# The four products after the gates with the tokens as the stationary operand and 512 weight columns moving

## The chip, the cores and the metric

The kernel runs on one core of one Trainium2 chip. The metric is device time in microseconds (us) of one execution; lower is better. In the text **PE** is TensorE, **PEld** its weight loads, **DVE** VectorE, **ACT** ScalarE, **SP** the queue that issues transfers. Lnnn is a line of the kernel before; where a line is one of the changed kernel, the text says so.

## The reference, cut to what matters

One block with 256 latent tokens and 256 context tokens, 2048 channels wide. All inputs are float32. The part that the change touches:

```python
u = hn @ w_in + b_in                      # 7 slices of 2048 columns: a, g, z_c, xr, z_r, gc, gr
y_conv = (swish(layernorm(conv(a * sigmoid(g)))) * silu(z_c)) @ w_conv_out
y_rnn = ((hf + hb) * silu(z_r)) @ w_rnn_out     # hf, hb: scans over the tokens, both directions
y = sigmoid(gc) * y_conv + sigmoid(gr) * y_rnn
out = rmsnorm(x + gt * (y @ w_o), final_g)      # gt: a gate vector from silu(c) @ w_ada
```

So five products of 256 tokens by a 2048 x 2048 matrix stand at the end: **gr** and **gc** (columns of w_in), **rnn** (w_rnn_out), **conv** (w_conv_out) and **o** (w_o). The four first feed the merge `y`, the fifth takes it.

## The kernel before

**Products.** A float32 product is made of three of the type float32r: each operand is split into a leading part and a remainder (`xh`, `xl` of the tokens, `whi`, `wlo` of the weights), and `whi*xh + whi*xl + wlo*xh` is summed in PSUM. A *block* is 1 MB of weights (two halves of 512 KB, tiles `raw`). `stage_load` asks for a block three ahead; `stage_split(s + 2, h)` makes `whi` on ACT (L180) for the block two ahead, and `wlo` on DVE (L185) for the half block before that one. There are four buffers of each kind, so a `whi` can be made only when PE has done the half block two blocks earlier.

**Two forms of a block.** In `slot` (L573, products at L234) a block is 128 output channels: 16 channel tiles of weights are stationary one after the other, the 256 tokens move, 48 products of 256 columns, and the result has the channels on the partitions. In the loop of w_o (L928, `o_mms`, products at L912) four blocks together make a *chunk* of 512 output columns: a 128 x 128 tile of the tokens is stationary, 512 weight columns move, 24 products per block, two sums (one per 128 tokens), and the result has the tokens on the partitions. The operand of either form has the channels on the partitions.

**Order.** After the first part (adaLN, the recurrent branch) the blocks run as a and g (32 blocks), z_c, gr, rnn, gc, conv, o (16 each). Everything is emitted in program order; each engine works through its own instructions in that order. DVE's other work is spread by hand: `side` is a list of closures with a cost in nominal us, and each half block runs `budget / 2` of it (`run_side`, L411). The list holds first the 480 taps of the depthwise convolution (L660), then LayerNorm (`ln_center`, `ln_a`, `ln_b`), then the 16 splits of the conv operand into `xh`, `xl` (`ln_split`, L774: ACT, then DVE), then four memsets of the gt sums (L763) and `gt_start`. What is left of the list after gc runs at once (L866 to L868). `gt_step` (L820, 64 of them) sums the vector gt on DVE from weights of its own (`gtraw`); its first step also needs a row `bgt`, loaded (L814) after the memsets.

**Results.** gr and gc go from PSUM through ACT's tanh with the bias as a per-partition operand (L851, L863); rnn is multiplied in by one DVE instruction per block (L855); conv by two (L875, L876), and the merged tile is split at once into `xh`, `xl` for w_o (L877). All of these are 128 x 256. The two last w_o blocks run one token tile after the other, and `finish` normalises and stores (L943 to L949).

Of the kernel before, what the change touches and what calls it, by code (L numbers as in the profile page):

```python
# [81 lines left out]
def block_kernel(ctx, tc, xcat, xtok, fgrow, par, wada, wgt, bgt, wearly, wall, wgate, out):  # L82
# [55 lines left out]
    # softplus(-lam) = max(-lam, 0) + log1p(exp(-|lam|)), log1p(e) = 2 atanh(e / (2 + e))  # L138
# [55 lines left out]
    def rsqrt(dst, tmp, src):  # L194
        # dst = (src + eps) ** -0.5, one Newton step on the table's value
# [7 lines left out]
    def ada_mms(acc, raw, rnd, n):  # L203
        # raw holds 8 // n channel tiles of 128 n columns of w_ada
# [7 lines left out]
    def ada_fin(row, part, k0, n):  # L212
        # sums of the four partial rows, channels to partitions
# [11 lines left out]
    def stat_mm(acc, x, i):  # L225
        # mean over channels: four column groups of the array take every fourth tile
# [10 lines left out]
    with ExitStack() as st:  # L237
# [28 lines left out]
        # with the tokens on the partitions, and back  # L266
# [27 lines left out]
        def products(m, ks, ws):  # L294
# [7 lines left out]
            # partial sums, in the end where the input's first tiles were  # L302
# [282 lines left out]
    s = 0  # L585
# [438 lines left out]
```

## Time and profile before

| | us |
|---|---|
| median of 3 runs | 1146.66 (1145.42 to 1146.89) |
| span of the profiled execution | 1142.0 |
| its own time | not listed apart from the span; the runs lie 3.4 to 4.9 above it |
| PE busy | 1121.5 |
| DVE busy | 924.9 |
| ACT busy | 615.1 |
| moved by transfers | 233.70 MB, mean 205 GB/s |

The span runs from the first to the last instruction that the profiler recorded. Busy times are of each engine alone and overlap. Two figures stand for the length of an instruction: the mean of one, in which neighbours on an engine can overlap, and the busy time over the count, in which they do not. PE is read best from the chain of waits, which gives pieces of uninterrupted work with their number of products.

### The profile page before, as it was taken

To read this page: it belongs to the slowest core of one execution; us is meant where nothing else is said; L and a number is where in the kernel's file an instruction comes from. 1 tells how busy PE (TensorE), PEld (TensorE's weight loads), DVE (VectorE), ACT (ScalarE), POOL (GpSimd) and SP (SyncE) were. 2 spreads that over 40 slices of the span, in tenths; PEclk is the share of its full clock that TensorE was granted. 3 is DMA by queue.
4 is the path that set the end of the run, shared out by engine and by line. 5 is a ranking of instruction groups with operands and counts; after the bars stand their busy time and mean duration, and the time that the engine had idled before them with its cause. 6 is when DMAs were issued, how large, how long until landed. Compare 5 with 4: busy or idle time off the path is not lost.

```text
span 1142.0 us, 20720 instructions
## 1 busy us (share of the span) xinstructions
PE 1121.5 (98%) x8316; PEld 1010.7 (88%) x8316; DVE 924.9 (81%) x1528; ACT 615.1 (54%) x838; POOL 0.2 (0%) x4
## 2 busy tenths in 40 slices
PE   6999999999999999999999999999999999999996
PEld 3777778777798989999999999999999999999885
DVE  5555588789879888899998989999985977888885
ACT  3222279777888877644454444443335854444443
POOL 0000000000000000000000000000000000000000
PEclk9999999999999999999999999999999999999999
DMA  9998444233346555465555555555554569888772
GB/s 376 400 409 324 189 134 134 102 125 125 106 141 196 160 167 164 143 209 184 185 185 171 183 183 185 175 183 178 181 188 150 169 205 324 316 310 285 268 279 93
DMA packets 67635, 233.70 MB, mean 205 GB/s; under 512 B 7505, under 2 KB 11729, under 8 KB 67153
## 3 DMA queue, kind: packets, MB, share of 16 engines
q1 hardware_dynamic: 67538, 232.37, 59.5%
q8 instruction: 65, 1.06, 0.4%
q14 instruction: 32, 0.26, 0.1%
HBM read 230.25 MB, written 2.10 MB: 203 GB/s over the span
## 4 chain that ended last, share of the span: by engine, by line
PE 98%; DVE 1%; DMA 0%; ACT 0%; issue 0%; ACTq 0%; SPq 0%; DVEq 0%
PE acc L234 72%; PE o L912 8%; PE xr L234 6%; PE gate L472 5%; PE ada L209 2%; PE part L234 2%; PE ms L228 1%; DMA hbuf<-in_xcat_dram 0%; PE tp L216 0%; PE mps L228 0%; PE gps L833 0%; PE vps L228 0%; DVE sq L259 0%; DVE wlo L171 0%; PE tot L279 0%
## 5 line engine op out<-in xcount | busy, mean ns | idle before, releaser
L234 PE MATMUL acc<-xh,whi 128*128 128x256 f32 (+1 forms) x2176 | 566.8, 296 | 0.0
L234 PE MATMUL acc<-xl,whi 128*128 128x256 f32 (+1 forms) x2176 | 552.3, 289 | 0.0
L180 ACT ACTIVATE whi<-raw 128x1024 fp32r<-128x1024 f32 x304 | 321.1, 1058 | 351.0 <-PE acc L234 277.3
L234 PEld LDWEIGHTS acc<-xh,whi 128*128 128x128 f32 x2176 | 416.7, 192 | 17.8 <-issue 9.3
L234 PEld LDWEIGHTS acc<-xl,whi 128*128 128x128 f32 x2176 | 416.9, 192 | 12.5 <-issue 7.7
L185 DVE TENSOR_TENSOR wlo<-raw,whi 128x1024 fp32r<-128x1024 f32 x304 | 371.0, 1223 | 70.0 <-ACT whi L180 66.3
L234 PE MATMUL acc<-xh,wlo 128*128 128x256 f32 (+1 forms) x2176 | 319.0, 289 | 0.0
L234 PEld LDWEIGHTS acc<-xh,wlo 128*128 128x128 f32 x2176 | 288.2, 192 | 5.0
L660 DVE SCALAR_TENSOR_TENSOR cv<-hbuf,pt,cv 128x196 f32<-128x196 f32 (+14 forms) x480 | 185.9, 451 | 13.0 <-ACT cv L651 12.6
L461 DVE SCALAR_TENSOR_TENSOR xc<-xr,pt,xc 128x510 f32<-128x510 f32 (+2 forms) x96 | 71.0, 742 | 0.2
L472 PE MATMUL gate<-xc,gw 128*128 128x512 f32 x128 | 60.0, 592 | 0.0
L820 DVE SCALAR_TENSOR_TENSOR zc<-gtraw,csil,zc 128x512 f32<-128x512 f32 x64 | 47.9, 748 | 5.4 <-DMA gtraw<-in_wgt_dram 4.7
L234 PE MATMUL xr<-xh,whi 128*128 128x512 f32 x96 | 40.4, 421 | 0.4 <-ACT xh L170 0.4
L912 PE MATMUL o<-whi,xh 128*128 128x512 f32 x128 | 40.6, 399 | 0.0
L498 DVE TENSOR_TENSOR_SCAN tr<-a,ti 128x512 f32<-128x512 f32 x32 | 39.1, 1223 | 0.7
L333 ACT ACTIVATE row<-ada 128x128 f32<-128x128 f32 (+1 forms) x22 | 7.2, 326 | 60.2 <-PE ada L209 60.2
L912 PE MATMUL o<-whi,xl 128*128 128x512 f32 x128 | 39.5, 389 | 0.0
L912 PE MATMUL o<-wlo,xh 128*128 128x512 f32 x128 | 39.4, 389 | 0.0
L234 PE MATMUL xr<-xl,whi 128*128 128x512 f32 x96 | 37.7, 392 | 0.2 <-DVE xl L171 0.2
L472 PEld LDWEIGHTS gate<-xc,gw 128*128 128x128 f32 x128 | 22.8, 189 | 17.0 <-issue 13.9
L234 PE MATMUL xr<-xh,wlo 128*128 128x512 f32 x96 | 37.4, 390 | 0.0
L209 PE MATMUL ada<-adaraw,csil 128*32 128x128 f32 (+1 forms) x704 | 32.5, 324 | 1.1 <-DVE sh L218 0.9
(169 smaller groups left out, 838.1 us busy)
## 6 DMA issues: line engine op xcount, KB each, us to landing
raw<-in_wall_dram SPq DMA_DIRECT2D x304, 512.0 KB, 3.5
adaraw<-in_wada_dram SPq DMA_DIRECT2D x64, 512.0 KB, 8.5
gtraw<-in_wgt_dram SPq DMA_DIRECT2D x32, 512.0 KB, 3.9
raw<-in_wearly_dram SPq DMA_DIRECT2D x16, 512.0 KB, 9.9
gw<-in_wgate_dram SPq DMA_DIRECT2D x32, 128.0 KB, 3.2
hbuf<-in_xcat_dram SPq DMA_DIRECT2D x2, 1024.0 KB, 7.1
cv<-in_xtok_dram SPq DMA_DIRECT2D x4, 512.0 KB, 5.8
out_dram<-cv SPq DMA_DIRECT2D x6, 256.0 KB, 2.6
```

Of the source, the lines that this page charges most:

```text
L180: A.activation(out=hi, in_=raw, func=AF.Copy)
L185: V.tensor_tensor(out=lo, in0=raw, in1=hi.bitcast(F32), op=SUB)
L209: PE.matmul(out=acc[g:g + 32, :w], lhsT=csil[:, k, :], rhs=raw[:, w * q:w * q + w], start=(k < 4), stop=(k >= KT - 4), tile_position=(0, g))
L228: PE.matmul(out=acc[32 * q:32 * q + 32, :], lhsT=ones[:, :32], rhs=x, start=(i < 4), stop=(i >= KT - 4), tile_position=(0, 32 * q))
L234: PE.matmul(out=acc, lhsT=w, rhs=x, start=(first and i == 0), stop=(last and i == n - 1))
L333: A.activation(out=row, in_=acc, func=AF.Copy)
L461: V.scalar_tensor_tensor(out=o, in0=i, scalar=w, in1=o, op0=MUL, op1=ADD)
L472: PE.matmul(out=acc, lhsT=u["gw"][:, c:c + 128], rhs=u["xc"], start=True, stop=True)
L498: V.tensor_tensor_scan(out=r(u["tr"]), data0=r(u["a"]), data1=r(u["ti"]), initial=0.0, op0=MUL, op1=ADD)
L660: V.scalar_tensor_tensor(out=o, in0=i, scalar=hdw[:, m * CW + j:m * CW + j + 1], in1=o, op0=MUL, op1=ADD)
L820: V.scalar_tensor_tensor(out=gt_chunk(c), in0=gt_raw[0][:, 512 * (k % 2):512 * (k % 2) + 512], scalar=csil[:, k, 0:1], in1=gt_chunk(c), op ...
L912: PE.matmul(out=acc, lhsT=y[:, k, 1, P * i:P * i + P], rhs=w[:, 512 * kk:512 * kk + 512], start=(k == 0 and w is hi and y is xh), stop=(k ...
```

## The change

gr, rnn, gc and conv take the form that w_o has: `chunk_mms` is the former `o_mms` with a choice of the operand's half, `chunk_slot` is `slot` with it, and `chunks` runs four chunks of four blocks. The weights of the four matrices are laid out for it outside the kernel's time. The gates and the merge then have the tokens on the partitions. The biases of gr and gc lie along the free axis now: they are loaded as rows spread over all partitions (`bias_load`, one buffer of 512 columns) and added on DVE before the tanh. The evacuations are 128 x 512, two per chunk. The merged value has to get back to channels on the partitions for w_o: `turn` makes two 128 x 128 transposes on PE into PSUM and splits from there. The budgets of side work go from 2.9 to 2.5 (gr, rnn) and from 2.6 to 2.3 (gc), and the squares of LayerNorm have 6 buffers instead of 8. The number of weight blocks, their splits and their loads are as before.

```diff
-BUD_XR, BUD_ZR, BUD_R, BUD, BUD_LN = 8.0, 2.7, 3.0, 2.9, 2.6
+BUD_XR, BUD_ZR, BUD_R, BUD, BUD_Y, BUD_LN = 8.0, 2.7, 3.0, 2.9, 2.5, 2.3
+GBB = 1
+CHUNKED = ("gr", "rnn", "gc", "conv", "o")
...
-    seq += [("in", BGR + m) for m in range(KT)]
-    seq += [("rnn", m) for m in range(KT)]
-    seq += [("in", BGC + m) for m in range(KT)]
-    seq += [("conv", m) for m in range(KT)]
-    seq += [("o", m) for m in range(KT)]
+    for a in CHUNKED:
+        seq += [(a, m) for m in range(KT)]
...
+    def chunk_mms(acc, s, seg, kq, h, i):
+        hi, lo = parts[s, h]
+        for w, y in ((hi, xh), (hi, xl), (lo, xh)):
+            for kk in range(2):
+                k = 4 * kq + 2 * h + kk
+                PE.matmul(out=acc, lhsT=y[:, k, seg, P * i:P * i + P], rhs=w[:, 512 * kk:512 * kk + 512],
+                          start=(k == 0 and w is hi and y is xh), stop=(k == KT - 1 and w is lo))
+    def chunk_slot(s, seg, accs, kq, budget):
+        stage_load(s + 3)
+        for h in range(2):
+            for i in range(2):
+                chunk_mms(accs[i], s, seg, kq, h, i)
+            del parts[s, h]
+            stage_split(s + 2, h)
+            run_deferred()
+            run_side(budget / 2)
...
-        sq = tp2.tile([P, T], F32, tag="sq", name="sq", bufs=8)
+        sq = tp2.tile([P, T], F32, tag="sq", name="sq", bufs=6)
...
-    for m in range(KT):
-        acc = slot(s, lat, T, BUD)
-        A.activation(out=p2[:, m], in_=acc, func=AF.Tanh, scale=0.5, bias=hbin[:, BGR + m:BGR + m + 1])
-        s += 1
-    for m in range(KT):
-        acc = slot(s, ctxp, T, BUD)
-        V.scalar_tensor_tensor(out=p2[:, m], in0=p2[:, m], scalar=1.0, in1=acc, op0=ADD, op1=MUL)
-        s += 1
+    p2v = p2.rearrange("p k t -> p (k t)")
+    tgv = vb.rearrange("p k t -> p (k t)")
+    def piece(v, c, i):
+        return v[:, 2048 * i + 512 * c:2048 * i + 512 * c + 512]
+    def bias_load(j, c):
+        t = tp2.tile([P, 512], F32, tag="gbias", name="gbias", bufs=GBB)
+        SP.dma_start(out=t, in_=bass.AP(brow.tensor, 2048 * j + 512 * c, [[0, P], [1, 512]]))
+        return t
+    def chunks(seg, budget, evac, before=None):
+        nonlocal s
+        for c in range(4):
+            accs = [psum(f"y{c}{i}") for i in range(2)]
+            for kq in range(4):
+                if before:
+                    before(c, kq)
+                chunk_slot(s, seg, accs, kq, budget)
+                s += 1
+            for i in range(2):
+                evac(c, i, accs[i])
+    def gate(v, c, i, acc, bias):
+        g = piece(v, c, i)
+        V.tensor_tensor(out=g, in0=acc, in1=bias, op=ADD)
+        A.activation(out=g, in_=g, func=AF.Tanh, scale=0.5)
+    gbias = {}
+    def before_gr(c, kq):
+        if kq == 1:
+            gbias[c] = bias_load(0, c)
+    chunks(1, BUD_Y, lambda c, i, acc: gate(p2v, c, i, acc, gbias[c]), before_gr)
+    def evac_rnn(c, i, acc):
+        g = piece(p2v, c, i)
+        V.scalar_tensor_tensor(out=g, in0=g, scalar=1.0, in1=acc, op0=ADD, op1=MUL)
+    chunks(0, BUD_Y, evac_rnn)
     ln["rnn"] = True
     ln_splits()
-    for m in range(KT):
-        acc = slot(s, lat, T, BUD_LN)
-        while m not in conv_done:
-            run_side(0.5)
-        A.activation(out=tgc[:, m], in_=acc, func=AF.Tanh, scale=0.5, bias=hbin[:, BGC + m:BGC + m + 1])
-        gt_steps(GTG)
-        s += 1
+    def before_gc(c, kq):
+        if kq == 1:
+            gbias[c] = bias_load(1, c)
+        gt_steps(GTG)
+    def evac_gc(c, i, acc):
+        while any(m not in conv_done for m in (8 * i + 2 * c, 8 * i + 2 * c + 1)):
+            run_side(0.5)
+        gate(tgv, c, i, acc, gbias[c])
+    chunks(1, BUD_LN, evac_gc, before_gc)
     while side or any(queue):
         run_side(1e9)
         run_deferred()
-    for m in range(KT):
-        acc = slot(s, ctxp, T, 0.0)
-        gt_steps(GTN)
-        if m % 2:
-            o_load(m // 2)
-        V.scalar_tensor_tensor(out=tgc[:, m], in0=tgc[:, m], scalar=1.0, in1=acc, op0=ADD, op1=MUL)
-        V.tensor_tensor(out=p2[:, m], in0=p2[:, m], in1=tgc[:, m], op=ADD)
-        split(xh[:, m, 1, :], xl[:, m, 1, :], p2[:, m])
-        s += 1
+    def turn(m):
+        tps = psum("tps")[:, :T]
+        for i in range(2):
+            PE.transpose(tps[:, P * i:P * i + P], p2v[:, 2048 * i + P * m:2048 * i + P * m + P], pall("ident"))
+        split(xh[:, m, 1, :], xl[:, m, 1, :], tps)
+    turns = deque()
+    def before_conv(c, kq):
+        gt_steps(GTN)
+        m = 4 * c + kq
+        if m % 2:
+            o_load(m // 2)
+        if turns:
+            turn(turns.popleft())
+    def evac_conv(c, i, acc):
+        g, t = piece(p2v, c, i), piece(tgv, c, i)
+        V.scalar_tensor_tensor(out=t, in0=t, scalar=1.0, in1=acc, op0=ADD, op1=MUL)
+        V.tensor_tensor(out=g, in0=g, in1=t, op=ADD)
+        if i:
+            turns.extend(range(4 * c, 4 * c + 4))
+    chunks(0, 0.0, evac_conv, before_conv)
...
-    def o_mms(acc, s, kq, h, i):
-        hi, lo = parts[s, h]
-        for w, y in ((hi, xh), (hi, xl), (lo, xh)):
-            for kk in range(2):
-                k = 4 * kq + 2 * h + kk
-                PE.matmul(out=acc, lhsT=y[:, k, 1, P * i:P * i + P], rhs=w[:, 512 * kk:512 * kk + 512],
-                          start=(k == 0 and w is hi and y is xh), stop=(k == KT - 1 and w is lo))
...
-                    o_mms(accs[i], s, kq, h, i)
+                    chunk_mms(accs[i], s, 1, kq, h, i)
                 del parts[s, h]
                 stage_split(s + 2, h)
                 gt_steps(GTO)
+                if turns:
+                    turn(turns.popleft())
```

The order of the instructions shows the change at three places. **DVE at the end of gc** (`xl<-cv` are the splits of the conv operand, `MEMSET zc` clears the sums of gt, L820, in the changed kernel L842, are gt's steps, L898 of the changed kernel adds gc's bias for the last chunk). Before:

```order
L171 TENSOR_TENSOR xl<-cv,xh 128x256 x3
L185 TENSOR_TENSOR wlo<-raw,whi 128x1024
L171 TENSOR_TENSOR xl<-cv,xh 128x256 x2
L763 MEMSET zc 128x512
L185 TENSOR_TENSOR wlo<-raw,whi 128x1024
L763 MEMSET zc 128x512 x2
L185 TENSOR_TENSOR wlo<-raw,whi 128x1024
L763 MEMSET zc 128x512
L185 TENSOR_TENSOR wlo<-raw,whi 128x1024
L820 SCALAR_TENSOR_TENSOR zc<-gtraw,csil,zc 128x512 x2
```

and now:

```order
L187 TENSOR_TENSOR wlo<-raw,whi 128x1024
L173 TENSOR_TENSOR xl<-cv,xh 128x256 x3
L898 TENSOR_TENSOR hbuf<-y_9185,gbias 128x512
L898 TENSOR_TENSOR hbuf<-y_9186,gbias 128x512
L173 TENSOR_TENSOR xl<-cv,xh 128x256 x13
L785 MEMSET zc 128x512 x4
L842 SCALAR_TENSOR_TENSOR zc<-gtraw,csil,zc 128x512 x2
L187 TENSOR_TENSOR wlo<-raw,whi 128x1024 x2
L842 SCALAR_TENSOR_TENSOR zc<-gtraw,csil,zc 128x512 x2
```

Before, the splits and memsets stood between the weights' remainders, a few at a time; now 13 splits, four memsets and two steps of gt stand in one run ahead of the next two remainders.

**PE between two conv blocks** (`acc` are the sums of two neighbouring blocks). Before:

```order
L234 MATMUL acc_10591<-xh,whi 128x256
L234 MATMUL acc_10591<-xl,whi 128x256
L234 MATMUL acc_10591<-xh,wlo 128x256 x8
L234 MATMUL acc_10660<-xh,whi 128x256
L234 MATMUL acc_10660<-xl,whi 128x256
```

and now, at the end of the first conv chunk (`y_9408` is its second sum, `y_9575` the first sum of the next chunk, `tps` the transposes, L936 of the changed kernel):

```order
L581 MATMUL y_9408<-whi,xh 128x512 x2
L581 MATMUL y_9408<-whi,xl 128x512 x2
L581 MATMUL y_9408<-wlo,xh 128x512 x2
L936 MATMUL tps<-pt,p_5033 128x128 x2
L581 MATMUL y_9575<-whi,xh 128x512 x2
L581 MATMUL y_9575<-whi,xl 128x512 x2
L581 MATMUL y_9575<-wlo,xh 128x512 x2
```

The next block's products followed directly; now the first two transposes, which read the merged chunk, stand ahead of the next chunk's products. The same stands at the two other chunk ends of conv; the other 13 pairs of transposes stand between blocks, or, after conv, between half blocks of w_o.

**DVE in the last w_o chunk** (ssq and ms are the norm's sums, L896 and in the changed kernel L974 the first instruction on a finished sum). Before:

```order
L896 SCALAR_TENSOR_TENSOR hbuf<-o_12056,zc 128x512
L897 TENSOR_TENSOR cv<-cv,hbuf 128x512
L899 TENSOR_TENSOR cv<-cv,zc 128x512
L901 TENSOR_TENSOR ms_11710<-ssq 128x1
L902 TENSOR_TENSOR ms_11710<-ms_11710,ssq 128x1
L185 TENSOR_TENSOR wlo<-raw,whi 128x1024 x5
L896 SCALAR_TENSOR_TENSOR hbuf<-o_12225,zc 128x512
L897 TENSOR_TENSOR cv<-cv,hbuf 128x512
```

and now:

```order
L842 SCALAR_TENSOR_TENSOR zc<-gtraw,csil,zc 128x512
L187 TENSOR_TENSOR wlo<-raw,whi 128x1024
L842 SCALAR_TENSOR_TENSOR zc<-gtraw,csil,zc 128x512
L187 TENSOR_TENSOR wlo<-raw,whi 128x1024
L842 SCALAR_TENSOR_TENSOR zc<-gtraw,csil,zc 128x512
L187 TENSOR_TENSOR wlo<-raw,whi 128x1024
L842 SCALAR_TENSOR_TENSOR zc<-gtraw,csil,zc 128x512 x4
L974 SCALAR_TENSOR_TENSOR hbuf<-o_10685,zc 128x512
```

Eight steps of gt, which were done by then, stand now between and behind the last five remainders (two remainders and two steps stand, in turn, ahead of the rows shown); the product over the partitions that ends gt (`gps`, L833) follows on PE when they are done, between the two token tiles of the last chunk.

## Rows read from the trace of the kernel before

**Rows 1.** The page: span, PE's busy time, and the chain by line.

```profile
span 1142.0 us, 20720 instructions
PE 1121.5 (98%) x8316; PEld 1010.7 (88%) x8316; DVE 924.9 (81%) x1528; ACT 615.1 (54%) x838; POOL 0.2 (0%) x4
...
PE acc L234 72%; PE o L912 8%; PE xr L234 6%; PE gate L472 5%; PE ada L209 2%; PE part L234 2%; PE ms L228 1%; DMA hbuf<-in_xcat_dram 0%; PE tp L216 0%; PE mps L228 0%; PE gps L833 0%; PE vps L228 0%; DVE sq L259 0%; DVE wlo L171 0%; PE tot L279 0%
```

**Rows 2.** The chain of waits in order of time: start us, us, what, number of instructions.

```profile
19.24 1.16 PE tot L279 x8
...
458.53 92.15 PE acc L234 x768
...
862.86 3.06 PE acc L234 x24
866.49 3.06 PE acc L234 x24
...
883.75 112.31 PE acc L234 x936
996.05 0.86 PE gps L833 x2
...
1077.37 43.56 PE o L912 x192
```

**Rows 3.** Windows over gr, gc and conv: each engine's busy us, clock, DMA.

```profile
641.00:733.00 92.00, 92.00 (x762) 90.36 (x761) 82.85 (x156) 41.40 (x52) 0.00 (x0) 1.00 0.57 182
...
825.00:918.00 93.00, 93.00 (x773) 89.62 (x772) 73.13 (x134) 54.76 (x84) 0.00 (x0) 1.00 0.54 171
918.00:1043.00 125.00, 125.00 (x1038) 124.52 (x1037) 102.64 (x141) 57.22 (x74) 0.00 (x0) 1.00 0.84 295
```

**Rows 4.** Groups by line: count, busy us, mean ns, idle before and its releaser.

```profile
L185 DVE TENSOR_TENSOR wlo<-raw,whi 128x1024 fp32r<-128x1024 f32 x304 | 371.0, 1223 | 70.0 <-ACT whi L180 66.3
...
L660 DVE SCALAR_TENSOR_TENSOR cv<-hbuf,pt,cv 128x196 f32<-128x196 f32 (+14 forms) x480 | 185.9, 451 | 13.0 <-ACT cv L651 12.6
...
L473 ACT ACTIVATE ti<-gate,hbi 128x512 f32<-128x512 f32 x32 | 22.0, 687 | 3.6 <-PE gate L472 3.2 <-DVE tr L498 0.2 <-DVE xc L461 0.2
```

**Rows 5.** Timeline of ACT and DVE in gr; in brackets idle before, and releaser.

```profile
705.36 1.06 ACT L180 ACTIVATE whi<-raw 128x1024 fp32r<-128x1024 f32 x1 [1.82 <-PE acc L234]
...
706.46 1.23 DVE L185 TENSOR_TENSOR wlo<-raw,whi 128x1024 fp32r<-128x1024 f32 x1 [0.58 <-ACT whi L180]
```

**Rows 6.** Timeline of ACT, DVE and SP around the end of gc.

```profile
915.50 1.32 ACT L170 ACTIVATE xh<-cv 128x256 fp32r<-128x256 f32 x4
...
915.94 1.43 DVE L171 TENSOR_TENSOR xl<-cv,xh 128x256 fp32r<-128x256 f32 x4 [0.65 <-ACT xh L170]
...
927.01 1.02 DVE L763 MEMSET zc<- 128x512 f32 x2
...
935.92 1.54 DVE L820 SCALAR_TENSOR_TENSOR zc<-gtraw,csil,zc 128x512 f32<-128x512 f32 x2 [4.66 <-DMA gtraw<-in_wgt_dram]
...
930.47 0.33 SPq L814 DMA_DIRECT2D zc<-in_bgt_dram x1
```

**Rows 7.** The page's transfers: KB each, median us from issue to landing.

```profile
gtraw<-in_wgt_dram SPq DMA_DIRECT2D x32, 512.0 KB, 3.9
...
out_dram<-cv SPq DMA_DIRECT2D x6, 256.0 KB, 2.6
```

**Rows 8.** Timeline of DVE and PE in the last w_o chunk and behind it.

```profile
1116.36 4.63 DVE L185 TENSOR_TENSOR wlo<-raw,whi 128x1024 fp32r<-128x1024 f32 x4
...
1127.38 0.69 DVE L896 SCALAR_TENSOR_TENSOR hbuf<-o,zc 128x512 f32<-128x512 f32 x1 [4.03 <-PE o L912]
...
1132.75 0.69 DVE L896 SCALAR_TENSOR_TENSOR hbuf<-o,zc 128x512 f32<-128x512 f32 x1 [0.79 <-PE o L912]
1133.47 0.69 DVE L897 TENSOR_TENSOR cv<-cv,hbuf 128x512 f32<-128x512 f32 x1
...
1120.77 1.02 PE L833 MATMUL gps<-zc,unit 128*128 128x512 f32 x2
```

More of the change, by code (lines that the diff above doesn't have):

```diff
@@ L72, in block_order, with block_kernel @@
     seq += [("in", BZC + m) for m in range(KT)]
-    seq += [("in", BGR + m) for m in range(KT)]
-    seq += [("rnn", m) for m in range(KT)]
-    seq += [("in", BGC + m) for m in range(KT)]
-    seq += [("conv", m) for m in range(KT)]
-    seq += [("o", m) for m in range(KT)]
+    for a in CHUNKED:
+        seq += [(a, m) for m in range(KT)]
     return seq
 @with_exitstack
-def block_kernel(ctx, tc, xcat, xtok, fgrow, par, wada, wgt, bgt, wearly, wall, wgate, out):
+def block_kernel(ctx, tc, xcat, xtok, fgrow, brow, par, wada, wgt, bgt, wearly, wall, wgate, out):
     nc = tc.nc
@@ L904, in last @@
     def last(i):
-        return p2[:, 2 * i:2 * i + 2].rearrange("p a t -> p (a t)")
-    def o_mms(acc, s, kq, h, i):
-        hi, lo = parts[s, h]
-        for w, y in ((hi, xh), (hi, xl), (lo, xh)):
-            for kk in range(2):
-                k = 4 * kq + 2 * h + kk
-                PE.matmul(out=acc, lhsT=y[:, k, 1, P * i:P * i + P], rhs=w[:, 512 * kk:512 * kk + 512],
-                          start=(k == 0 and w is hi and y is xh), stop=(k == KT - 1 and w is lo))
+        return piece(p2v, 0, i)
     def finish(i):
@@ L946, in block_kernel @@
             for h in range(2):
-                o_mms(accs[i], s + q, 2 + q, h, i)
+                chunk_mms(accs[i], s + q, 1, 2 + q, h, i)
         evac_o(3, i, accs[i])
@@ L985, in tiles, with chunked @@
         return w.reshape(KT, P, -1, P).transpose(2, 1, 0, 3)
-    mats = {"in": tiles(i["w_in"][0]), "conv": tiles(i["w_conv_out"][0]), "rnn": tiles(i["w_rnn_out"][0])}
-    wo = i["w_o"][0].reshape(4, 2, 2, P, 4, 512).transpose(4, 0, 1, 3, 2, 5).reshape(KT, 2, P, 1024)
-    wall = np.stack([wo[m] if a == "o" else mats[a][m].reshape(P, 2, 1024).transpose(1, 0, 2)
+    def chunked(w):
+        return w.reshape(4, 2, 2, P, 4, 512).transpose(4, 0, 1, 3, 2, 5).reshape(KT, 2, P, 1024)
+    win = i["w_in"][0]
+    mats = {"in": tiles(win), "gr": chunked(win[:, P * BGR:]), "gc": chunked(win[:, P * BGC:P * BGR]),
+            "rnn": chunked(i["w_rnn_out"][0]), "conv": chunked(i["w_conv_out"][0]), "o": chunked(i["w_o"][0])}
+    wall = np.stack([mats[a][m] if a in CHUNKED else mats[a][m].reshape(P, 2, 1024).transpose(1, 0, 2)
                      for a, m in block_order()])
@@ L996, in _pack @@
     wgate = g.transpose(2, 3, 0, 1, 4).reshape(KT, P, 512)
-    return {"xcat": xcat, "xtok": i["x"][0].reshape(OUT), "fgrow": i["final_g"].reshape(1, -1), "par": par,
+    return {"xcat": xcat, "xtok": i["x"][0].reshape(OUT), "fgrow": i["final_g"].reshape(1, -1),
+            "brow": np.concatenate([i["b_in"][:, P * BGR:], i["b_in"][:, P * BGC:P * BGR]], axis=1), "par": par,
             "wada": wada, "wgt": wgt, "bgt": i["b_ada"][:, 4096:], "wearly": wearly, "wall": wall, "wgate": wgate}
```

## The prediction

> **What bounds the kernel now.** I read the page first: PE is busy 1121.5 of 1142.0 us, and the chain by line is PE almost alone, 72% of it the products of L234 and 8% those of w_o [rows 1]. The chain in time order then gives the price of work without a gap. In the form of `slot`, 768 products (16 blocks) take 92.15, so 5.76 a block; in w_o's form 192 products (8 blocks) take 43.56, so 5.445. A half block alone takes 2.88 of the first and 2.72 of the second [rows 2]. The windows tell what else is near its limit: in gr DVE is busy 82.85 of 92, in gc DVE 73.13 and ACT 54.76 of 93, in conv DVE 102.64 of 125 with the transfers at 0.84; PE's clock is 1.00, so no clock is to be won there [rows 3]. DVE's waits are nearly all for `whi` (66.3 of 70.0 before `wlo`) [rows 4], and `whi` itself waits for PE (idle 1.82 of a half block), since it needs a buffer that PE has to leave [rows 5]. So ACT and DVE run behind PE, about a block ahead of need. A shorter PE shortens the kernel until one of them, or an order, lacks that block. Every term below is one of PE's time: a chain that is 98% PE has nothing else to shorten.
>
> **The change, part by part.**
>
> 1. *Saving.* 64 blocks go from 5.76 to 5.445 [rows 2]: 64 x 0.314 = **-20.1**. Both prices are from uninterrupted rows, so I give this no range.
>
> 2. *One more pass of statistics.* With six buffers for squares the sums of LayerNorm come in six groups, not five. Such a group lies between two half blocks: 862.86 to 866.49 is 3.63 instead of 2.88 [rows 2]. **+0.75**.
>
> 3. *Transposes.* 16 pairs are new on PE, and no row shows one. Lower end: two products at the shortest pitch, 2.88/24 = 0.12 each, 0.24 a pair. Upper end: a pair like one fp32 product of `gps`, 0.86/2 = 0.43. Between them lie eight small fp32 products in 1.16, 0.29 for two [rows 2]. I take the middle, 0.34. At three chunk ends the first of a pair lies in a wait that is counted next, so 13 x 0.34 + 3 x 0.17 = **+4.9** (3.5 to 6.2).
> The Trainium skill, "TensorE: Matmul & The Clock Gate", Part 4: PE-mode transpose, speaks against the change here: some 275 ns for one 128 x 128 transposition of bf16 within a kernel. By it the term would be an estimated 13 x 0.55 + 3 x 0.275 = 8.0 and the time 1153.2; no row here shows a transposition.
>
> 4. *Waiting for the turn.* At the end of conv's chunks 0, 1 and 2 PE's next instruction is a transpose of the merged chunk, ahead of 24 products that need nothing from it. It needs four DVE instructions of 128 x 512, at the pitch of the norm's instructions, 1133.47 - 1132.75 = 0.72 [rows 8]. Let E be the end of the chunk's last product. The `whi` of the half block before is made when that half ends, E - 2.7, takes 1.06 and is followed by 1.23 of `wlo` [rows 5], so DVE is held to E - 0.2. Then 4 x 0.72: E + 2.7. Three times: **+8.1**. Lower end 1.5 each (first sum evacuated during the last half of the second, two instructions left), 4.5; upper end another `wlo` ahead, 3.9 each, 11.8. Queued behind the waiting transpose are all of PE's products; ACT's next `whi` waits for them in turn, so nothing is gained back.
>
> 5. *The pile at the end of gc.* The smaller budget leaves 13 splits of the conv operand, four memsets and the start of gt undone when gc ends, and they are emitted at once, ahead of two `wlo`. Prices: a split 1.32/4 = 0.33 on ACT and 1.43/4 = 0.36 on DVE, two memsets 1.02, two gt steps 1.54 [rows 6]; tanh of 128 x 512 0.69 with overlap [rows 4]; a transfer like `bgt` 2.6, that of the 256 KB stores [rows 7]. From E, the end of gc's last product: `whi` gets its buffer and is done at 1.3; three splits on ACT to 2.3, on DVE to 2.7; two bias additions to 4.1; tanh to 4.8; 13 splits to 9.1, on DVE 9.5; memsets 11.5; `bgt`, asked for behind the memsets, lands 14.1; two gt steps, which need it, 15.6; `wlo` 16.9. PE meanwhile: conv can start at 1.7 (first split), waits 0.6 for the fourth, ends block 0 at 7.7, the first half of block 1 at 10.5, 0.9 of products of the next half that need no `wlo` at 11.4, and waits until 16.9. 1.7 + 0.6 + 5.5 = **+7.8**. Lower end: `bgt` lands at no cost, 5.2. Upper end: its landing takes the 3.9 of a `gtraw` [rows 7], 9.1. Before, the same start of gt cost DVE 4.66 of waiting at 935.92 [rows 6] and PE nothing, since two remainders stood ahead of it.
>
> 6. *The tail.* The last w_o chunk starts 10.9 (two blocks) ahead of `gps`, 1120.77 - 10.9 = 1109.9 = c. Now `gps` stands behind the first token tile of the last two blocks (c + 16.3) and needs eight gt steps. DVE is free at c + 6.5 (1116.36), makes five `wlo` (4.63 + 1.2) [rows 8] and eight steps of 0.77 [rows 6]: c + 18.5. With `gps` at 0.86 and the second tile at 5.45, PE ends at c + 24.8; before it ended at c + 22.8 (the last sum is taken up at 1132.75) [rows 8]. **+2.0**, lower end 0.
>
> *At nothing:* the bias rows (eight of 256 KB, 2.6 each [rows 7]) are asked for three blocks ahead of use. The bias additions and the taps stay on DVE under PE if DVE keeps within a block: in gr 82.85/16 = 5.18 [rows 3], less one tap of 0.387 (185.9/480 [rows 4]) by the budget, plus two additions in four blocks, 2 x 0.69/4 = 0.35: 5.1 of 5.445. In gc, 73.13 [rows 3] plus some 28 taps left over from earlier (10.8) and eight additions (5.5) is 89.4, of a stretch that is now 16 x 5.445 plus about 5 of statistics, 92. That cover is thin; if it goes, rival B gives the price.
>
> Sum: -20.1 + 0.75 + 4.9 + 8.1 + 7.8 + 2.0 = **+3.45**. The profiled execution has a span of 1142.0 [rows 1], and the runs shown lie 3.4 to 4.9 above it; the sum is of differences within that span, so span 1145.45, and on the median 1146.66 + 3.45 = **1150.1**. All lower ends together: -6.15, 1140.5. All upper ends: +9.75, 1156.4.
>
> **Rivals.**
>
> *A, the pile is hidden: faster.* If ACT and DVE reach the end of gc with more of a lead than I gave them, or the stretch of 16.9 shrinks below PE's 11.4, the whole term 5 falls away: 1150.1 - 7.8 = 1142.3. It decides the sign from the point at which the pile costs under 2.1 (below 1144.4, 0.2% under the median). For it: before, the very same splits cost PE nothing, and ACT is busy only 54.76 of 93 in gc [rows 3]. Against it: the order of the instructions, in which two `wlo` stand behind a transfer that stands behind 13 splits.
>
> *B, DVE becomes the bound in gr, rnn and gc: slower.* At 5.1 of 5.445 DVE has 0.3 a block, 1.3 a chunk, and the two instructions at each chunk's end come as one burst of 1.4. If each burst makes one `wlo` late by what the lead can't take, say 0.5 in each of 12 chunks, it costs 6: 1156. It decides once DVE needs over 5.445 a block. For it: the thin margins above. Against it: before, DVE still waited in gr (0.58 ahead of a `wlo`) [rows 5].
>
> *C, the transposes go at the pitch of the shortest products.* Then term 3 is 3.5 and the time 1148.7: within 0.2%.
> The same page of the Trainium skill, section Terms, says that trn2's transpose mode is four times as fast for fp32; that would be this case. No run here shows it yet.
>
> *D, the change doesn't do what it says.* If 128 tokens as stationary operand gave no better pitch in these four than `slot` has, because the two halves of the tokens are read from other places than in w_o, the saving is gone: 1170. Against it: operands, shapes and counts are those of w_o's products.
>
> **How the numbers follow.** The kernel's runs lie within 1.5 us; a difference of 0.2% (2.3) is about what can be told from none. Forecast with its middle sizes, 1149 to 1152: 0.32. C, and the forecast with a turn or a pile nearer to its lower end, 1144.4 to 1149: 0.30. A: 0.20. B, or the upper ends: 0.15. D: 0.03. So faster 0.2 (A), same 0.3, slower 0.5. The range begins at A's 1142 and ends at 1156, at B and the sum of upper ends; D, the far side of A, and what lies past the upper ends make some 0.2 together. The likeliest side's own range is 1149 to 1156.
>
> **What would show it.** Right: half blocks of gr, rnn, gc and conv at 2.72; PE idle some 2.7 for DVE ahead of the first transpose at three places in conv; about 5 idle in the second conv block while DVE waits for `bgt`; pairs of transposes near 0.34; `gps` waiting for DVE in the last chunk; DVE's idle time in gr still ending with `whi`. Wrong: no idle PE after gc (A); PE waiting for `wlo` inside gr or rnn (B); a half block still at 2.88 (D).

## The result

The changed kernel takes 1152.91 us in the median (1152.36 to 1154.81), the kernel before 1146.04 beside it: a ratio of 1.0065, interval [1.0054, 1.0077], so 0.65% slower, where +0.3% was forecast. The profiled execution is the slowest of the four, 1153.0 of span and 1154.81 of time.

The page of the changed kernel (span, busy time, chain by line) answers to [rows 1]:

```profile
span 1153.0 us, 17738 instructions
...
PE 1116.5 (97%) x6812; PEld 937.0 (81%) x6812; DVE 929.9 (81%) x1520; ACT 611.2 (53%) x822; POOL 0.2 (0%) x4
...
PE acc L236 40%; PE y L581 29%; PE xr L236 6%; PE gate L474 5%; PE o L581 3%; PE ada L211 3%; PE part L236 2%; DMA raw<-in_wall_dram 2%; DVE zc L842 1%; DVE wlo L187 1%; PE ms L230 1%; ACT whi L182 1%; PE tp L218 0%; DMA hbuf<-in_xcat_dram 0%; PE mps L230 0%
```

PE does less work than before (1116.5 for 1121.5), and holds 89% of the chain instead of 98%; loads of weights and DVE have come into it. The windows tell where (columns as in [rows 3]; stage bounds are found by counting products in the chain). Before, the rows are gr to gc, conv, and o:

```profile
665.00:950.00 285.00, 285.00 (x2364) 279.44 (x2364) 240.59 (x440) 138.59 (x188) 0.00 (x0) 1.00 0.57 184
950.00:1043.00 93.00, 93.00 (x771) 92.52 (x771) 80.68 (x112) 41.29 (x50) 0.00 (x0) 1.00 0.89 315
1043.00:1133.00 90.00, 89.71 (x390) 72.86 (x389) 67.92 (x91) 39.32 (x52) 0.00 (x0) 1.00 0.62 219
```

and now:

```profile
668.10:938.80 270.70, 270.70 (x1208) 217.38 (x1207) 234.93 (x417) 129.72 (x154) 0.00 (x0) 1.00 0.61 192
938.80:1049.70 110.90, 96.64 (x412) 76.75 (x412) 83.86 (x114) 44.47 (x65) 0.00 (x0) 0.95 0.76 268
1049.70:1144.00 94.30, 90.98 (x399) 73.48 (x397) 75.27 (x102) 40.61 (x55) 0.00 (x0) 1.00 0.66 226
```

gr to gc gained 285.0 - 270.7 = 14.3. conv lost 17.9, o about 4. Another 3 us of the difference of the two spans lie before gr (668.1 against 665.0), in code that the change doesn't touch: from 20 to 40 us the granted clock of PE was 0.76 in this execution and 1.00 in the one before. They belong to the execution and not to the change: in the runs below, with the same code there, gr starts between 665.1 and 668.0. In conv PE is idle for 14.3 of 110.9, and its clock falls to 0.95, though in gr to gc all is as forecast: the chain there has blocks without a gap (216 products in 49.19, 5.466 a block) and half blocks of 2.95 with 0.56 of statistics between them, in six groups:

```profile
740.18 49.19 PE y L581 x216
...
885.23 2.95 PE y L581 x12
888.17 0.56 PE vps L230 x6
```

What PE waited for in all, from gr on (us in total, times, longest):

```profile
PE tps L936 <- DVE p L952: 8.0, 6, 4.0
PE y L581 <- DVE wlo L187: 4.8, 1, 4.8
PE gps L855 <- DVE zc L842: 3.1, 1, 3.1
PE y L581 <- ACT xh L172: 1.5, 1, 1.5
```

PE's timeline shows the three gaps at the start of conv (in brackets the idle time before, and the releaser):

```profile
940.27 0.80 PE L581 MATMUL y<-whi,xh 128*128 128x512 f32 x2 [1.45 <-ACT xh L172]
...
949.63 0.61 PE L581 MATMUL y<-whi,xl 128*128 128x512 f32 x2
955.02 1.22 PE L581 MATMUL y<-wlo,xh 128*128 128x512 f32 x2 [4.77 <-DVE wlo L187]
956.04 1.05 PE L581 MATMUL y<-whi,xh 128*128 128x512 f32 x2
956.89 1.05 PE L581 MATMUL y<-whi,xl 128*128 128x512 f32 x2
...
958.76 0.61 PE L581 MATMUL y<-whi,xl 128*128 128x512 f32 x2
...
968.73 0.61 PE L581 MATMUL y<-wlo,xh 128*128 128x512 f32 x2
973.39 0.48 PE L936 MATMUL tps<-pt,p 128*128 128x128 f32 x1 [4.05 <-DVE p L952]
974.72 0.47 PE L936 MATMUL tps<-pt,p 128*128 128x128 f32 x1 [0.84 <-DVE p L952]
```

The last product of gc ends at 938.8. PE starts conv 1.45 later, runs out of `wlo` at 950.2, stands 4.77, finishes the first chunk at 969.2 and stands for the transposes until 974.7. Behind the long gap two products start 0.85 after the two before (956.04, 956.89) instead of 0.46, and the granted clock from 955.02 to 957.74 was 0.50: that is the lower of the clock's two levels, 1.2 GHz. The ten from 955.02 to 958.76 took 3.74 instead of 2.28, 1.5 on top of the gap. Behind the second gap the chain has a whole block at 7.05 instead of 5.47, 1.6 on top (granted clock 0.76 from 974.84 to 982.2); behind the waits at the next chunk end a block takes 5.48. A pair of transposes between products stands there at 0.22:

```profile
975.19 7.05 PE y L581 x24
982.24 0.22 PE tps L936 x2
...
1001.54 5.48 PE y L581 x24
```

What PE waited for at the two gaps is seen on DVE, SP's queue and ACT, in this order:

```profile
948.28 2.11 DVE L785 MEMSET zc<- 128x512 f32 x4
952.29 1.54 DVE L842 SCALAR_TENSOR_TENSOR zc<-gtraw,csil,zc 128x512 f32<-128x512 f32 x2 [1.91 <-DMA zc<-in_bgt_dram]
953.74 2.36 DVE L187 TENSOR_TENSOR wlo<-raw,whi 128x1024 fp32r<-128x1024 f32 x2
...
970.79 1.23 DVE L187 TENSOR_TENSOR wlo<-raw,whi 128x1024 fp32r<-128x1024 f32 x1
971.93 0.68 DVE L951 SCALAR_TENSOR_TENSOR hbuf<-hbuf,y 128x512 f32<-128x512 f32 x1
```

```profile
950.41 0.30 SPq L836 DMA_DIRECT2D zc<-in_bgt_dram  x1
953.86 0.35 SPq L830 DMA_DIRECT2D gtraw<-in_wgt_dram  x1
954.32 1.04 SPq L177 DMA_DIRECT2D raw<-in_wall_dram  x2
```

```profile
958.91 1.06 ACT L182 ACTIVATE whi<-raw 128x1024 fp32r<-128x1024 f32 x1 [9.58 <-DMA raw<-in_wall_dram]
```

DVE's memsets and the landing of `bgt` come ahead of `wlo` at 953.74, as the prediction had it. What it had not is the lack of weights behind it. SP's queue issues nothing for 11.1 us, because the load of `bgt` (950.41) waits for the memsets; the next load of gt (953.86) waits for DVE's first step, and the next weight loads stand behind it (954.32). There is a second reason, which run 5 below shows: a weight load needs one of four `raw` buffers, and DVE's late `wlo` is what frees them. ACT then stands 9.58 for weights, `wlo` of the first chunk's last half block comes only at 970.79, and the merge (971.93) behind that.

In the last w_o chunk DVE's steps and SP's loads are:

```profile
1127.55 0.74 DVE L842 SCALAR_TENSOR_TENSOR zc<-gtraw,csil,zc 128x512 f32<-128x512 f32 x1
...
1131.14 0.75 DVE L842 SCALAR_TENSOR_TENSOR zc<-gtraw,csil,zc 128x512 f32<-128x512 f32 x1
...
1135.56 1.54 DVE L842 SCALAR_TENSOR_TENSOR zc<-gtraw,csil,zc 128x512 f32<-128x512 f32 x2 [1.08 <-DMA gtraw<-in_wgt_dram]
```

```profile
1128.32 3.93 SPq L830 DMA_DIRECT2D gtraw<-in_wgt_dram  x2
```

gt has two buffers, and a step of DVE frees one: the last two loads of gt go out as such steps end, at 1128.32 and 1131.92. The last lands 3.54 later; DVE stands 1.08 for it, its last two steps end at 1137.1, and only then can `gps` start.

### The profile page after: what moved, and what is told of

Same layout as the page of the kernel before. It is cut to its first block, busy times and chain, and to the rows that moved or that the text cites. A ratio compares the mean times of both kernels' runs of the same rounds, so it can differ in the third digit from the quotient of the medians.

```text
span 1153.0 us, 17738 instructions
## 1 busy us (share of the span) xinstructions
PE 1116.5 (97%) x6812; PEld 937.0 (81%) x6812; DVE 929.9 (81%) x1520; ACT 611.2 (53%) x822; POOL 0.2 (0%) x4
## 4 chain that ended last, share of the span: by engine, by line
PE 89%; DVE 4%; DMA 3%; ACT 1%; issue 1%; SPq 0%; ACTq 0%; DVEq 0%
PE acc L236 40%; PE y L581 29%; PE xr L236 6%; PE gate L474 5%; PE o L581 3%; PE ada L211 3%; PE part L236 2%; DMA raw<-in_wall_dram 2%; DVE zc L842 1%; DVE wlo L187 1%; PE ms L230 1%; ACT whi L182 1%; PE tp L218 0%; DMA hbuf<-in_xcat_dram 0%; PE mps L230 0%
## 5 line engine op out<-in xcount | busy, mean ns | idle before, releaser
L236 PE MATMUL acc<-xh,whi 128*128 128x256 f32 (+1 forms) x1152 | 313.8, 306 | 0.0
L236 PE MATMUL acc<-xl,whi 128*128 128x256 f32 (+1 forms) x1152 | 301.1, 295 | 0.0
L236 PEld LDWEIGHTS acc<-xh,whi 128*128 128x128 f32 x1152 | 220.3, 191 | 13.4 <-issue 7.0
L236 PEld LDWEIGHTS acc<-xl,whi 128*128 128x128 f32 x1152 | 220.5, 191 | 12.2 <-issue 7.4
L236 PE MATMUL acc<-xh,wlo 128*128 128x256 f32 (+1 forms) x1152 | 175.3, 295 | 0.0
L581 PE MATMUL y<-wlo,xh 128*128 128x512 f32 x512 | 159.1, 392 | 4.8 <-DVE wlo L187 4.8
L581 PE MATMUL y<-whi,xh 128*128 128x512 f32 x512 | 162.2, 398 | 1.5 <-ACT xh L172 1.5
L236 PEld LDWEIGHTS acc<-xh,wlo 128*128 128x128 f32 x1152 | 156.1, 192 | 5.0
L581 PE MATMUL y<-whi,xl 128*128 128x512 f32 x512 | 159.0, 392 | 0.0
L581 PEld LDWEIGHTS y<-wlo,xh 128*128 128x128 f32 x512 | 96.8, 189 | 25.5 <-DVE wlo L187 5.2
L842 DVE SCALAR_TENSOR_TENSOR zc<-gtraw,csil,zc 128x512 f32<-128x512 f32 x64 | 47.9, 748 | 3.7 <-DMA zc<-in_bgt_dram 1.9
```

Source lines behind the costliest of these rows:

```text
L236: PE.matmul(out=acc, lhsT=w, rhs=x, start=(first and i == 0), stop=(last and i == n - 1))
L581: PE.matmul(out=acc, lhsT=y[:, k, seg, P * i:P * i + P], rhs=w[:, 512 * kk:512 * kk + 512], start=(k == 0 and w is hi and y is xh), stop=( ...
L842: V.scalar_tensor_tensor(out=gt_chunk(c), in0=gt_raw[0][:, 512 * (k % 2):512 * (k % 2) + 512], scalar=csil[:, k, 0:1], in1=gt_chunk(c), op ...
```

## The experiments

Each run has the kernel before beside it on the same chip; ratios are to that. Three edits recur: **L**, transposes later; **G**, side work earlier, so that gt starts ahead of conv; **P**, gt's loads on POOL's queue.

**1. The transposes one block later (L).**

```diff
     def before_conv(c, kq):
...
-        if turns:
-            turn(turns.popleft())
+        for _ in range(min(len(turns), (0, 1, 1, 2)[kq])):
+            turn(turns.popleft())
```

> The transposes of a conv chunk begin one block later: none ahead of a chunk's first block, one pair ahead of the second and third, two ahead of the fourth. Nothing else changes. Theory (the transposes that stand ahead of a chunk's products hold PE until DVE has merged the chunk): the three waits of the changed kernel's trace go, 5.5 us at the first chunk end and about 2.1 at each of the two others, and with the first also some 2.0 us of products at a lower clock behind it; about -11.6, so 1141 us. Rival (the first of the three is a lack of weights, because loads came late, and would only move to the next weight remainder): -4.3, so 1148.6 us.

Measured: 1149.18 us, ratio 1.0041 [1.0027, 1.0055], so 0.24% better than the changed kernel. In the trace PE's waits for the transposes fell from 8.0 to 0.6 us and conv from 110.9 to 99.7, much as the theory had it. But the profiled execution (1142.89) is the fastest of ten that reach up to 1152.33, and in the median the gain is 2.7 us, below the rival's 4.3. What the slower executions lost again no trace shows, so the rival is neither confirmed nor refuted.

**2. Side work in gc at 3.0 instead of 2.3.**

```diff
-BUD_XR, BUD_ZR, BUD_R, BUD, BUD_Y, BUD_LN = 8.0, 2.7, 3.0, 2.9, 2.5, 2.3
+BUD_XR, BUD_ZR, BUD_R, BUD, BUD_Y, BUD_LN = 8.0, 2.7, 3.0, 2.9, 2.5, 3.0
```

> The budget of side work in gc is 3.0 instead of 2.3 nominal us per block, so that the 16 splits and the four memsets stand between the weight remainders ahead of gc's end. Theory (the pile at the end of gc holds PE twice, and its transfer of bgt holds the weight loads behind it on SP's queue): the idle 1.45 + 4.77 us go, with 1.9 us of slow products behind them, and the first chunk end falls from 5.5 + 2.0 us to the 2.1 of the others; the tail gains 1 to 3 because gt starts earlier. About -13 to -16, so 1137 to 1140 us. Rival (DVE has no room for more in gc, and remainders come late inside gc): gc grows by about what the end of gc gains, 1148 to 1153 us.

Measured: 1150.87 us, ratio 1.005 [1.0034, 1.0066]. The pile is gone, and PE's waits for `xh` and `wlo` behind gc fell from 6.3 to 2.0; but the wait at the first chunk end grew to 6.6 (the three ends: 10.6 instead of 8.0). Inside gc PE has no wait, and gc took 92.7 instead of 93.7. So the theory missed; the time lies in the rival's range, but not for its reason. The cost moved. Two pieces of the timelines of DVE and of SP's queue in this run:

```profile
946.23 1.54 DVE L842 SCALAR_TENSOR_TENSOR zc<-gtraw,csil,zc 128x512 f32<-128x512 f32 x2 [3.50 <-DMA gtraw<-in_wgt_dram]
```

```profile
941.62 0.30 SPq L836 DMA_DIRECT2D zc<-in_bgt_dram  x1
947.79 0.35 SPq L830 DMA_DIRECT2D gtraw<-in_wgt_dram  x1
948.25 1.10 SPq L177 DMA_DIRECT2D raw<-in_wall_dram  x2
```

The start of gt still falls on the border of gc and conv. DVE waits 3.50 for gt's first load; the third load of gt waits for DVE's steps; the weights (948.25) wait behind it. While SP stood so, from 941.9 to 947.8, it issued nothing.

**3. Each transpose twice.**

```diff
-        for i in range(2):
+        for i in (0, 1, 0, 1):
             PE.transpose(tps[:, P * i:P * i + P], p2v[:, 2048 * i + P * m:2048 * i + P * m + P], pall("ident"))
```

> Each transpose of the merged value is made twice, the second over the first: 32 more on PE. By the trace of the changed kernel (two transposes in 0.22 us between products) +16 x 0.22 = +3.5, so 1156.4 us. If a transpose cost the 0.27 us each that the Trainium skill states (TensorE: Matmul & The Clock Gate, Part 4: PE-mode transpose), +8.8, so 1161.7 us. The price that the prediction took, 0.34 for two, gives +5.4, 1158.3 us.

Measured: 1155.41 us, ratio 1.0103 [1.0077, 1.0129], 0.38% or 4.3 us above the changed kernel, with an interval of some 3 us. In the chain four transposes stand at 0.44. So 0.11 each: 3.5 for 32. What one takes from its start to its end is more. In the changed kernel (ns, min/median/max):

```profile
L936 PE MATMUL tps<-pt,p x32: 270/271/476, 973.4 to 1062.1; 128*128 128x128 f32 x32
```

The Trainium skill (TensorE: Matmul & The Clock Gate, Part 4: PE-mode transpose) states some 275 ns for bf16 within a kernel. The trace agrees with it as the duration of one, 271 ns here. But neighbours on PE overlap, and what a transpose adds to the chain is 0.11; the expectation's +8.8, and the 8.0 that the prediction worked out beside its term, took the duration for the price.

**4. The memsets and the start of gt behind two conv blocks.**

```diff
-            side.extend((0.6, lambda c=c: V.memset(gt_chunk(c), 0.0)) for c in range(4))
-            side.append((0.0, gt_start))
...
     def before_conv(c, kq):
+        if (c, kq) == (0, 2):
+            for n in range(4):
+                V.memset(gt_chunk(n), 0.0)
+            gt_start()
```

> The memsets of gt and its start (two loads, the row bgt) move from the end of gc to the third conv block; the 13 splits stay where they are. Theory (in the pile it is the part behind the splits, memsets, the landing of bgt, two steps of gt, 5.6 us ahead of the weight remainder, that makes PE wait, and the row bgt on SP's queue that makes the next weight loads late): the idle 4.77 us and 1.5 us of slow products behind it go, and the first chunk end falls by 3.1 + 2.0 us; gt then ends four steps later, +2 to +4 in the tail. About -7 to -9, so 1144 to 1146 us. Rival (the 13 splits alone are enough): the stall stays at about 3 us, 1150 to 1153 us.

Measured: 1158.03 us, ratio 1.0117 [1.0099, 1.0135]. Half of it came as the theory said: behind gc PE has no wait for `wlo` any more, so the 13 splits alone don't make the 4.8 of the pile, and the rival is wrong. The one wait for `wlo` that is left stands behind gt's start at its new place:

```profile
960.18 0.88 PE L581 MATMUL y<-wlo,xh 128*128 128x512 f32 x2 [1.88 <-DVE wlo L187]
```

But the longest wait at a chunk end stayed (4.3 instead of 4.0), and `gps` in the last chunk waited 8.3 instead of 3.1. At this place, too, gt's start makes `wlo` late, and it ends later: of the two directions, back is the wrong one.

**5. gt's loads on POOL (P).**

```diff
-        SP.dma_start(out=raw, in_=wgt[n])
+        nc.gpsimd.dma_start(out=raw, in_=wgt[n])
...
-        SP.dma_start(out=gtb[0:1, :], in_=bgt)
+        nc.gpsimd.dma_start(out=gtb[0:1, :], in_=bgt)
```

> The changed kernel, with the 32 loads of gt's weights and the row bgt issued by POOL, which has nothing else to do, instead of SP. Theory (on SP's queue the loads of gt wait for DVE's steps and hold up the weight loads behind them, so that whi comes late in conv and the last loads of gt come late in turn): the first chunk end falls from 5.5 + 2.0 us to the 2.1 of the others, and the tail's wait of 3.7 us goes; the pile's 4.8 us stay, since the order on DVE is the same. About -9, so 1144 us. Rival (the transfers themselves are at their limit in conv, 360 GB/s, and the queue doesn't matter): no change, 1151 to 1154 us.

Measured: 1156.05 us, ratio 1.0098 [1.0078, 1.0117]: no gain, rather 0.3% worse. The longest wait at a chunk end fell from 4.0 to 2.3, as the theory said; but the pile's wait for `wlo` rose to 5.4 and that of `gps` to 3.9. The weights still come late. This is what SP's queue waits for between 930 and 975, and ACT's wait there:

```profile
SPq L177 <- DVE wlo L187: 33.7, 10, 14.6
```

```profile
956.69 1.06 ACT L182 ACTIVATE whi<-raw 128x1024 fp32r<-128x1024 f32 x1 [9.69 <-DMA raw<-in_wall_dram]
```

With gt's loads out of the way a weight load stands 14.6 for the `wlo` behind the pile, which frees its `raw` buffer, and ACT waits 9.69 where it waited 9.58. So the queue alone is not what holds this kernel. From 940 to 1145 DVE waits 6.2 us for gt's weights instead of 1.1; whether that makes the 0.3% is not tested.

**6. Side work 2.8 in gr and rnn, 3.0 in gc (G).**

```diff
-BUD_XR, BUD_ZR, BUD_R, BUD, BUD_Y, BUD_LN = 8.0, 2.7, 3.0, 2.9, 2.5, 2.3
+BUD_XR, BUD_ZR, BUD_R, BUD, BUD_Y, BUD_LN = 8.0, 2.7, 3.0, 2.9, 2.8, 3.0
```

> Side work 2.8 instead of 2.5 nominal us per block in gr and rnn and 3.0 instead of 2.3 in gc, so that not only the splits but also the start of gt comes some three blocks ahead of gc's end, about where the kernel before has it. Transposes as in the changed kernel. Theory (raising gc's budget alone left gt's first loads and the weight loads behind them at the start of conv; with both ahead of conv nothing is late there): the idle 6.2 and slow 1.9 us after gc go, the first chunk end falls by 5 to the 2.1 of the others, the tail's 3.7 go: about -16, so 1136 to 1139 us. Rival (DVE has no room for it in gr and rnn): those matrices and gc grow from 88.5 and 93.7 us by 1 to 3 each, 1141 to 1146 us.

Measured: 1145.01 us, ratio 0.9994 [0.9984, 1.0005]: 0.71% better than the changed kernel, and level with the kernel before. PE's wait for `gps` is gone, that for `wlo` is 1.9. The time lies in the rival's range, but its reason holds for gc alone: gr and rnn did not grow (192 products still take 43.75), gc went from 93.7 to 96.5, 1.9 of it that wait. The gain is half of what was expected; the waits for the transposes are 6.2 us still.

**7. G and L together.**

> The two together: side work as in the run before this one in the list, and the transposes of a chunk one block later. Theory (the turn's waits and the late weights are separate costs): another -6 from the three chunk ends, about 1130 to 1133 us, and faster than the kernel before by some 12. Rival (what the turns leave free the loads of conv take up, with 1 MB of weights, 512 KB of gt and 256 KB of the tokens in a block of 5.5 us): at most -2, 1135 to 1138 us.

Measured: 1140.03 us, ratio 0.9949 [0.9931, 0.9967]. L is worth 0.45% here, 5 us, about what was expected, from a level that was higher. PE still waits 3.5 for transposes and 2.3 for `wlo`. The chain in order of time goes round in a loop in conv (start, length, what):

```profile
963.14 5.99 DMA raw<-in_wall_dram
...
969.23 1.07 ACT whi L182
...
970.32 1.23 DVE wlo L187
971.55 0.67 DVE zc L842
...
972.24 0.75 DVE zc L842
...
973.93 9.07 DMA raw<-in_wall_dram
```

A weight load lands, `whi` is made, `wlo` and DVE's two steps of gt follow; only then does SP pass gt's next load and issue the next weights, which take 6 to 9 us to land. No engine fills such a loop: each round is a load's landing and what DVE has to do before SP may go on.

**8. G, L and P.**

> The same as the run before it in the list, with gt's loads issued by POOL as well. Theory (once gt starts early, SP's queue holds nothing up for long): no change against that run, within 2 us. Rival (the queue costs in steady state too, since in each block a weight load stands behind a load that waits for DVE): -3 to -5 us against that run.

Measured: 1132.57 us, ratio 0.9885 [0.9866, 0.9905], 0.64% below the run before. The rival is right: the queue costs in steady state. The loop is gone from the chain; conv is PE alone, at a granted clock of 1.00:

```profile
930.39 34.75 PE y L581 x152
965.14 0.22 PE tps L936 x2
```

**9. L and P without G**, and **10. G and P without L.**

> The changed kernel with the transposes one block later and gt's loads on POOL; side work as in the changed kernel, so the pile after gc stays. Theory (three causes, each with its own price: pile, turn, queue): the pile's idle 6.2 and slow 1.9 us, and some 3 us of the late gt in the tail, are what parts this from the version with all three, so 1143 to 1145 us. Rival (only turn and queue matter once DVE is free of the turn; the pile is made up for later): within 3 us of the version with all three, 1132 to 1136 us.

> The changed kernel with side work 2.8 and 3.0 and gt's loads on POOL; transposes as in the changed kernel. Theory (the turn's waits of about 2.1 us at three chunk ends are what is left): the version with all three plus 6.4, so 1139 us. Rival (without the later transposes the weights stay late too, as on SP's queue): 1143 to 1146 us, as with gt on SP.

Measured: 1148.36 us, ratio 1.0025 [1.0009, 1.0042], and 1140.51 us, 0.9952 [0.9936, 0.9968]. Without G the waits behind gc (5.4 and 1.1) and that of `gps` (5.1) are back, and it is 1.4% above all three, some 16 us where 10 to 12 were expected: the theory's direction, not its size. Without L the waits for transposes are 4.8 us, and it is 0.67% above, as expected. Both rivals fall.

**11. The kernel before with P.**

> The kernel before, with gt's loads and the row bgt on POOL and nothing else changed. Theory (before, PE has work at all times, so that a weight load that comes later is covered): no change, within 0.2% of the kernel before. Rival (the queue's wait costs the kernel before as well, and the gain of the last version is not the change's): -4 to -8 us.

Measured: 1145.82 us, ratio 1.0001 [0.9992, 1.0011]. The queue costs the kernel before nothing, so what P gives behind G and L is not to be had from P without the change.

**12. All three, and gt's first step three half blocks later.**

```diff
     def gt_start():
...
-        gt_todo.extend(range(4 * KT))
+        defer(3, lambda: gt_todo.extend(range(4 * KT)))
```

> The version with all three (early gt, later transposes, gt's loads on POOL), with gt's first step put off by three half blocks, so that DVE doesn't stand for the landing of bgt (4.9 us of waiting there at 927.66, and PE idle 1.94 behind it). Theory: the idle 1.9 us go, -2 against that version, 1130 to 1131 us. Rival (gt ends 1.5 blocks later and holds the last chunk's product): +2 to +4 in the tail, 1132 to 1136 us.

Measured: 1130.69 us, ratio 0.9877 [0.985, 0.9904]. PE's only wait left from gr on is 0.7 for `gps`. Against run 8 the difference is within the intervals, so the 2 us are seen in the trace and not proved by the times. This is the fastest version, 1.2% below the kernel before.

The eight cases in one table, ratio to the kernel before:

| | without P | with P |
|---|---|---|
| the change | 1.0065 | 1.0098 |
| L | 1.0041 | 1.0025 |
| G | 0.9994 | 0.9952 |
| G and L | 0.9949 | 0.9885 |

G is worth 0.7% alone, 0.9% with L and 1.4 to 1.5% with P; L 0.24% alone and 0.45 to 0.72% with one or both of the others; P nothing alone (0.3% worse), 0.2% with L and 0.4 to 0.6% with G. Alone they add up to 0.6%, together they give 1.8%: the three costs hide one another. That PE's wait for one of them gives the other two time is the likely reading; no run tests it apart.

## Why the prediction was right, and where it was wrong

The sign and the kind were right: the saving in the four matrices is there, and conv and the tail give back more than that. The sum was +3.45, the medians show +6.9. With the sizes below the terms add up to some +8 in the trace, and with the 3 us before gr to the 11.0 by which the two spans differ. Terms 1, 3 and 5 came near their size, and the errors of 1 and 3 cancel by luck (18.8 and 3.2 instead of 20.1 and 4.9); what the sum lacks is in terms 4 and 6.

*1. Saving.* Forecast 20.1; with blocks at 5.466 it is 64 x 0.294 = 18.8. Right but for 0.02 a block.

*2. Statistics.* Six groups of 3.51 instead of five of 3.63, as forecast; +0.9 for 0.75.

*3. Transposes.* 0.22 a pair, at the lower end (case C's price): 13 x 0.22 + 3 x 0.11 = 3.2, or 1.7 less than the term.

*4. The turn.* The second chunk end cost 2.1 (its last two products start at 998.71 and take 0.46 by their pitch; the next block's first starts at 1001.30), the third about as much, against 2.9 forecast with the transposes. The first cost 5.7 (969.2 to 974.84) and 1.6 of slow products. This is the step that failed: it took the remainder ahead of the merge to be on time ("DVE is held to E - 0.2"). In the trace that `wlo` starts at 970.79, 1.6 behind E, because its weights are late. They are late for two reasons: loads stood on SP's queue behind `bgt` and gt, and loads stood for a buffer that `wlo` behind the pile frees. Of the 4.9 that PE waits for the transposes at this chunk end (4.05 + 0.84), P alone took 1.6, G alone 1.1 and both 2.6 (runs 5, 6 and 10), which leaves 2.3, where the other two ends of the changed kernel have 1.6. So the queue is a part of it at this place and not the whole; in the steady part of conv runs 7 and 8, which differ in it alone, show its price.

*5. The pile.* Forecast `wlo` at 16.9 behind the end of gc and PE's halt at 11.4; in the trace 16.2 (first product of `wlo` at 955.02) and 11.4 (950.2). Forecast idle 7.8, measured 1.45 + 4.77 = 6.2, and 1.5 of slow products, which no term had; that the two make 7.7 is luck. Run 4 confirms that it takes the part behind the splits. "Asked for behind the memsets" was followed on DVE but not on SP's own queue, where two weight loads were next, nor to the `raw` buffers that the late `wlo` frees.

*6. The tail.* Forecast +2.0 by DVE's steps; o grew by some 4.4, of which 0.9 are four pairs of transposes and 3.1 the wait for `gps`. The mechanism is the one named, DVE's steps behind its remainders, undersized: the term has no landing of gt's last loads, each of which waits for a step that frees its buffer. SP's queue is not the cause here: with gt's loads on POOL `gps` waited 3.9 (run 5). With gt started earlier the wait is gone (run 6).

*Rivals.* A was wrong about the hidden pile. B was wrong: within gr, rnn and gc PE has no wait, and with budgets of 2.8 and 3.0 gr and rnn still ran at 43.75 for eight blocks. C was right about the transposes (3.2, it had 3.5), but other terms outweighed it. D was wrong: the blocks run at 5.466 instead of 5.76.

One reading of the trace was at fault, too. By its count of products the kernel before starts gr at 665, gc at 853 and conv at 950, so the windows of [rows 3] start 24, 28 and 32 us early, and [rows 6] does not stand at gc's end. These are gc's tanh and conv's first evacuation of the kernel before (count, ns min/median/max, first and last start):

```profile
L863 ACT ACTIVATE hbuf<-acc,hbin x16: 450/456/473, 861.7 to 950.3; 128x256 f32<-128x256 f32 x16
L875 DVE SCALAR_TENSOR_TENSOR hbuf<-hbuf,acc x16: 412/421/422, 955.8 to 1043.0; 128x256 f32<-128x256 f32 x16
```

So gc ended at 950, and the kernel before began gt (935.92, [rows 6]) two and a half blocks before that. So there was time left in gc, and "two remainders stood ahead" need not be the reason why it cost PE nothing. DVE also spent less there between two remainders: 7.35 us (from 930.03 to 937.38), against 14.4 in the changed kernel (939.34 to 953.74); run 6, with 7.5, kept a wait of 1.9. Which of these counts for how much was not tested apart. Read so, the row would have told what runs 2 and 6 showed: it matters in which stage gt starts.

## What to carry to other kernels

When a step is moved towards a busier stage, follow each of its transfers on the queue that issues it and to the buffer that it needs: a load that waits for a compute step holds up every load behind it, and in a stage whose transfers are busy nearly all the time (a DMA share of 0.86 in run 7's conv) this closes a loop of landing, split and step that no busy share shows. Costs that hide one another have to be removed together: here each edit alone gave -0.7 to +0.3%, all three 1.8%. And before a gain on the bounding engine is written off, look whether its losses are waits that the order makes; a delay of one block took nearly all of the transposes' wait away (8.0 to 0.6 us).

## What the hardware showed that was not expected

A transpose of 128 x 128 fp32 on TensorE lasted 0.271 us from start to end, but added only 0.11 us between products, no more than the shortest product of 256 columns (0.12). After PE's idle gaps of 4.8 and 5.7 us (the second broken by a transpose) its products ran at a pitch of 0.43 instead of 0.227, at 1.2 GHz, and cost 1.5 and 1.6 us more; after two gaps of under 1 us with a transpose between them, ahead of 1001.54, the next block took 5.48, so there the clock did not fall. The length of the wait alone does not tell: behind 1.87 us in run 6 the granted clock from 934 to 936 was 0.50, behind 1.94 us in run 8 it was 1.00 from 930.4 to 934. So a wait can cost more than its length, and two waits of one length can cost differently.
